# Four of eight channel tiles of a depthwise convolution: taps from VectorE to GpSimd

## The chip, the cores and the metric

One core of a Trainium2 chip runs the whole kernel. The metric is the device time of one execution in microseconds; lower is better. The engines are TensorE (PE in the profile; its weight loads are PEld), VectorE (DVE), ScalarE (ACT), GpSimd (POOL) and SyncE (SP). Each works through its own queue of instructions in order; semaphores order them against each other.

## The reference

One encoder layer on 512 tokens of width 1024, in float32:

```python
h = rms_norm(x, norm_mix_pre)
za, zb, q, k, v, su, sv, gl = split(h @ w_in)
a = za * sigmoid(zb)                          # the gated input of the convolution
a = depthwise_conv(a, conv_w, conv_b)         # 31 taps along the tokens, one filter a channel
y_a = silu(layer_norm(a, conv_ln_g, conv_ln_b)) @ w_proj_conv
y_b = rms_norm(diff_attention(q, k, v)) @ w_proj_attn        # 8 heads, two softmaxes each
y_c = (gelu(su) * spatial(layer_norm(gelu(sv)))) @ w_proj_sgu
g_a, g_b, g_c = split(sigmoid(gl + b_gate))
x = x + rms_norm((g_a*y_a + g_b*y_b + g_c*y_c) @ w_out)
x = x + rms_norm(relu(rms_norm(x) @ w_ffn_up)**2 @ w_ffn_down)
```

## The kernel before

All matrices are multiplied in three products of split operands: each float32 operand is a rounded part (`_hi`, written by ScalarE, L150) and the rest (`_lo`, subtracted by VectorE, L151), and hi x hi, hi x lo and lo x hi are summed. A *unit* is one 128 x 512 result over 1024 inputs: 24 products. Weights come by SyncE's queue, are split two units ahead of their use (`take`, `load_to`) and are kept in three buffers.

The order of TensorE is the order of the program (`keep_in_program_order`). The other engines' queues are ordered when the kernel is built, by a planner that follows dependences and a priority, which is the place in the program unless it is changed.

The stages that matter here, in TensorE's order:

1. The rows of x are normalized and turned; the first gated tiles (`glu`, 0 and 1) are made.
2. Attention, eight heads. A head makes scores for four groups of 128 tokens, and for each VectorE writes the combined probabilities `at` (L515); TensorE turns them, and ScalarE and VectorE split them into `ath` and `atl` (L72), which the product with the values reads. Between these steps run the next head's queries and keys (`kk`, L465) and the other six gated tiles (2 to 7).
3. The normalized and gelu'd half of the spatial gating unit (`sv_half`, `gv_norm`), with its two rows `sg_g` and `sg_b` and its weights `wraw` loaded through GpSimd's queue; the projection of attention; the spatial gating unit, which writes `sh` and `sl`; its projection, which reads them.
4. The convolution's norm (`conv_norm`: TensorE turns `apad`, ScalarE writes the normalized rows `y`), its silu, its projection, which writes `mh` and `ml`; then the output product and the feed-forward half.

The convolution has the channels on partitions, in eight tiles of 128 channels: `apad` holds a tile's 512 tokens with 15 zeros on either side. VectorE writes a gated tile into it (`glu_out`, L396). A tile's convolution is 31 instructions on VectorE, one after the other on one accumulator: the last tap with the bias (L367), then 30 fused multiply-and-add instructions (L372), the last of which writes over the start of the tile's own row. They are one generator over all tiles, `taps`; `conv(n, behind)` issues the next n of them after a given instruction, with a priority lowered by 3000. `glu_out` asks for 11 taps (`CONVG`), later hooks for 5, 14, 3 and 9 at a time.

Buffers named by the same tag in the same pool share a place. `sh` and `mh` are both `bh` in the pool `brp`; `y` has four buffers of its own in `p3`.

Of the kernel before, what the change touches and what calls it, by code (L numbers as in the profile page):

```python
# [8 lines left out]
F32 = mybir.dt.float32  # L9
F32R = mybir.dt.float32r  # L10
AF = mybir.ActivationFunctionType
ALU = mybir.AluOpType
# [4 lines left out]
P = 128  # L17
S = 512
D = 1024
KT = D // P  # L20
TT = S // P
# [3 lines left out]
CK = 31  # L25
PAD = 15
# [12 lines left out]
CONVG = 11  # L39
# [9 lines left out]
def encoder_layer(ctx: ExitStack, tc: tile.TileContext, a: dict, out: bass.AP):  # L49
    nc = tc.nc  # L50
    vec, act, pool = nc.vector, nc.scalar, nc.gpsimd
# [12 lines left out]
    def mk(name, bufs=1, **kw):  # L64
        return tc.tile_pool(name=name, bufs=bufs, reuse_waits="tile", **kw)
# [104 lines left out]
    def bank(tag):  # L170
        return ps["pool"].tile([P, 512], F32, tag=tag, bufs=ps[tag], name=f"ps_{tag}")
# [97 lines left out]
    with mk("p0") as p0:  # L269
# [76 lines left out]
        convw = cq.tile([P, KT, 32], F32, tag="convw", name="convw")  # L346
        vec.tensor_copy(convw, b[:, P:P + KT * 32].rearrange("p (k j) -> p k j", j=32))

        def pc(n, i=0):
            return pcol[:, col[n] + i:col[n] + i + 1]  # L350
# [6 lines left out]
    cvp = big.enter_context(mk("cvp"))  # L357
    apad = cvp.tile([P, KT, S + 2 * PAD], F32, tag="apad", name="apad")
# [2 lines left out]
    pad(big, "pad3", 64)  # L361
    mixp = big.enter_context(mk("mixp"))

    def conv_taps():
        for c in range(KT):
            acc = cvp.tile([P, S], F32, tag="acc", name="acc")
            vec.tensor_scalar(acc, apad[:, c, CK - 1:CK - 1 + S], convw[:, c, CK - 1:CK], pc("conv_b", c),  # L367
                              op0=ALU.mult, op1=ALU.add)
            yield
            for j in range(CK - 2, -1, -1):  # L370
                o = acc if j else apad[:, c, 0:S]
                vec.scalar_tensor_tensor(o, apad[:, c, j:j + S], convw[:, c, j:j + 1], acc,  # L372
                                         op0=ALU.mult, op1=ALU.add)
                yield

    taps = conv_taps()

    def conv(n, behind):

        with tc.issue_after(behind.ins):  # L380
            keep = tc.cur_priority
            tc.cur_priority = keep + LOWP
            for _ in range(n):
                next(taps, None)
            tc.cur_priority = keep + (tc.cur_priority - keep - LOWP)
# [7 lines left out]
        return sg  # L393

    def glu_out(c, ba, sg):
        conv(CONVG, vec.tensor_tensor(apad[:, c, PAD:PAD + S], ba, sg, op=ALU.mult))  # L396

    def glu(c, p):
        wb, wa = take(2)
        bb = bank("a")  # L400
        yield from unit_gen(bb, wb, hT)
        sg = glu_gate(bb, p)
        ba = bank("a")
        yield from unit_gen(ba, wa, hT)
        glu_out(c, ba, sg)

    glu_out(0, fb[1], glu_gate(fb[0], ap_))
    sg1 = glu_gate(fb[2], ap_)
    (w,) = take(1)
    b = bank("a")  # L410
    unit(b, w, hT)
    glu_out(1, b, sg1)
    for c in range(2, KT - GLU_LATE):
        run(glu(c, ap_))
# [3 lines left out]
    for i in (1, 2):  # L418
        lq = bcast(ap_, f"lq{i}", a[f"lam_q{i}"], 64)
        lk = bcast(ap_, f"lk{i}", a[f"lam_k{i}"], 64)  # L420
        pr = ap_.tile([P, 64], F32, tag="lpr", name="lpr")
# [164 lines left out]
    brp = big.enter_context(mk("brp"))  # L586
# [28 lines left out]
    bh = brp.tile([P, KT, S], F32R, tag="bh", name="bh")  # L615
# [17 lines left out]
    def ln_stats(p, parts):  # L633
        st = p.tile([P, 2, 6], F32, tag="st", bufs=4, name="st")
        for i, s in enumerate(parts):
            vec.bn_stats(st[:, i], s)
        mv = p.tile([P, 2], F32, tag="mv", bufs=4, name="mv")
        vec.bn_aggr(mv, st)
        r = rstd_of(p, mv[:, 1:2], 1.0)
        nb = p.tile([P, 1], F32, tag="nb", bufs=4, name="nb")  # L640
        vec.scalar_tensor_tensor(nb, mv[:, 0:1], -1.0, r, op0=ALU.mult, op1=ALU.mult)
        return mv, r, nb
# [96 lines left out]
    p3 = c3.enter_context(mk("p3"))  # L739
    ch = p3.tile([P, KT, S], F32R, tag="ch", name="ch")  # L740
    cl = p3.tile([P, KT, S], F32R, tag="cl", name="cl")
    ys = []

    def conv_norm(t):
        bs = [bank("b") for _ in range(2)]
        for c in range(KT):
            pe.transpose(bs[c // 4][:, (c % 4) * P:(c % 4 + 1) * P], apad[:, c, t * P:(t + 1) * P], ident)
        mv, r, nb = ln_stats(p3, bs)
        y = p3.tile([P, D], F32, tag="y", bufs=4, name="y")
        for i in range(2):  # L750
            act.activation(y[:, i * 512:(i + 1) * 512], bs[i], AF.Identity, bias=nb, scale=r)  # L751
        ys.append(y)

    def conv_silu(c):
        b = bank("b")
# [9 lines left out]
    for n in range(EARLY):  # L765
        (wg,) = take(1)
        ga.append(gate(p3, wg, 0, n, "ga", EARLY))
        if NORM <= n < NORM + 2:
            conv_norm(2 * (n - NORM))
            conv_norm(2 * (n - NORM) + 1)  # L770
        elif NORM + 2 <= n < NORM + 4:
            for c in range(4 * (n - NORM) - 8, 4 * (n - NORM) - 4):
                conv_silu(c)
# [377 lines left out]
    for q in range(1, FT // 4):  # L1151
# [15 lines left out]
        ba = bank("a")  # L1167
# [48 lines left out]
    ba = [bank("a") for _ in range(2)]  # L1216
# [45 lines left out]
    for n, step in enumerate(seq[:-TAIL]):  # L1262
# [4 lines left out]
        p_, i = step  # L1267
# [48 lines left out]
def build(arrays):  # L1316
    import concourse.bacc as _bacc

    nc = _bacc.Bacc("TRN2", target_bir_lowering=False, num_devices=1)
    args = {}  # L1320
    for n in _INS:
        a = arrays[f"in_{n}_dram"]
        args[n] = nc.dram_tensor(f"in_{n}_dram", a.shape, mybir.dt.from_np(a.dtype), kind="ExternalInput").ap()
    out = nc.dram_tensor("out_0_dram", (S, D), F32, kind="ExternalOutput").ap()
    with tile.TileContext(nc) as tc:
        encoder_layer(tc, args, out)
    return nc
# [10 lines left out]
```

## Time and profile before

| | us |
|---|---|
| Median of 3 runs | 1060.08 (1059.95 to 1060.1) |
| The profiled execution | 1059.99 |
| Its span, first to last instruction | 1058.2 |
| Busy: PE / DVE / ACT / POOL | 1042.6 / 827.0 / 580.5 / 24.3 |
| All taps of L372 that write the accumulator, 232 | 173.5 |
| First and last gated tile written (L396) | 38.7 and 307.8 |
| First transpose of `apad` | 597.8 |

In the profile's rows a time is followed by the engine, the line of the kernel, the operation and `out<-in` by the program's names, with the shapes; in brackets stands how long the engine had been idle and what it waited for. A row by stretch gives the stretch, its length, and busy time with the number of instructions of PE, PEld, DVE, ACT and POOL, then the granted clock, the share of the DMA engines and their GB/s; where it was asked for one line of the kernel it has that engine's time alone. A row of a line's instructions gives the shortest, median and longest duration in ns and the first and last start.

### The profile page before, as it was taken

How to read it: one execution, taken by the hardware profiler on the slowest of the kernel's cores; microseconds unless marked ns; L12 is line 12 of the kernel's file. 1: busy time of each engine (PE TensorE's matmuls, PEld its weight loads, DVE VectorE, ACT ScalarE, POOL GpSimd, SP SyncE). 2: the span in 40 equal slices, each digit the busy share in tenths (PEclk: the TensorE clock that was granted, in tenths of full speed). 3: DMA queues.
4: the chain of work that ended last, by engine and by line, in shares of the span. 5: the costliest groups of instructions: out<-in, count | busy, mean ns of one | idle time of the engine just before them, and what ended most of it. 6: DMA issues, size and time to landing. Idle time of an engine off the chain costs nothing.

```text
span 1058.2 us, 14724 instructions
## 1 busy us (share of the span) xinstructions
PE 1042.6 (99%) x5688; PEld 900.0 (85%) x5688; DVE 827.0 (78%) x1296; ACT 580.5 (55%) x902; POOL 24.3 (2%) x41
## 2 busy tenths in 40 slices
PE   8999999999999999999999999999999999999997
PEld 7989898888878888888888888888999999888885
DVE  6696887968997697999899546457988889867746
ACT  5456677766673752344322493344677787555531
POOL 3000000000000000000000000000000001100000
PEclk9999999999999999999999999999999999999999
DMA  7342323223232333322333214463343319724532
GB/s 227 84 139 61 100 81 100 80 81 87 73 120 87 92 112 90 99 81 80 100 100 99 80 45 135 132 226 138 112 150 101 122 43 265 150 80 139 178 121 80
DMA packets 138391, 118.15 MB, mean 112 GB/s; under 512 B 4166, under 2 KB 116850, under 8 KB 138321
## 3 DMA queue, kind: packets, MB, share of 16 engines
q1 hardware_dynamic: 133120, 103.82, 32.1%
q0 software_dynamic: 4480, 11.82, 4.8%
q10 hardware_dynamic: 720, 1.57, 0.4%
q8 instruction: 44, 0.72, 0.3%
q14 instruction: 27, 0.21, 0.1%
HBM read 108.81 MB, written 4.19 MB: 107 GB/s over the span
## 4 chain that ended last, share of the span: by engine, by line
PE 91%; DVE 5%; ACT 2%; issue 1%; DMA 1%; DVEq 0%; ACTq 0%
PE ps_a L58 69%; PE ps_b L58 19%; PE ps_b L62 3%; DVE w_lo L951 1%; DMA xx<-in_x_dram 1%; DVE us L1257 0%; DVE w_lo L151 0%; ACT y L751 0%; DVE hs L303 0%; DVE jk L827 0%; PE ps_a L62 0%; DVE hl L224 0%; ACT jk L825 0%; DVE jk L1247 0%; DVE rs_s L206 0%
## 5 line engine op out<-in xcount | busy, mean ns | idle before, releaser
L150 ACT ACTIVATE w_hi<-w_raw 128x1024 fp32r<-128x1024 f32 x116 | 122.9, 1059 | 214.0 <-PE ps_a L58 177.4
L58 PE MATMUL ps_a<-hh,w_hi 128*128 128x512 f32 (+1 forms) x536 | 205.4, 385 | 0.0
L58 PE MATMUL ps_a<-hh,w_lo 128*128 128x512 f32 (+1 forms) x536 | 202.9, 381 | 0.0
L58 PE MATMUL ps_a<-hl,w_hi 128*128 128x512 f32 (+1 forms) x536 | 202.5, 380 | 0.0
L372 DVE SCALAR_TENSOR_TENSOR acc<-apad,convw,acc 128x512 f32<-128x512 f32 x232 | 173.5, 748 | 5.0
L151 DVE TENSOR_TENSOR w_lo<-w_raw,w_hi 128x1024 fp32r<-128x1024 f32 x116 | 141.5, 1220 | 41.5 <-ACT w_hi L150 41.2
L58 PEld LDWEIGHTS ps_a<-hh,w_lo 128*128 128x128 f32 x536 | 100.3, 188 | 19.6
L58 PEld LDWEIGHTS ps_a<-hl,w_hi 128*128 128x128 f32 x536 | 100.4, 188 | 18.3
L58 PEld LDWEIGHTS ps_a<-hh,w_hi 128*128 128x128 f32 x536 | 100.4, 188 | 18.2
L58 PE MATMUL ps_a<-ring,w_hi 128*128 128x256 f32 x336 | 57.9, 276 | 0.0
L58 PEld LDWEIGHTS ps_a<-ring,w_hi 128*128 128x128 f32 x336 | 50.6, 188 | 0.0
L58 PE MATMUL ps_a<-h2h,w_lo 128*128 128x256 f32 x176 | 48.8, 277 | 1.4 <-DVE w_lo L951 1.4
L58 PE MATMUL ps_a<-w_hi,hh 128*128 128x256 f32 (+1 forms) x160 | 49.7, 311 | 0.0
L58 PE MATMUL ps_a<-h2h,w_hi 128*128 128x256 f32 x176 | 49.0, 278 | 0.0
L58 PE MATMUL ps_a<-h2l,w_hi 128*128 128x256 f32 x176 | 48.8, 277 | 0.0
L58 PE MATMUL ps_a<-w_hi,hl 128*128 128x256 f32 (+1 forms) x160 | 48.7, 304 | 0.0
L58 PE MATMUL ps_a<-w_lo,hh 128*128 128x256 f32 (+1 forms) x160 | 48.6, 304 | 0.0
L507 ACT ACTIVATE e<-ps_b,m 128x512 f32<-128x512 f32 x64 | 43.4, 681 | 7.3 <-DVE m L503 7.0
L58 PE MATMUL ps_a<-ring,w_lo 128*128 128x256 f32 x168 | 46.5, 277 | 0.2 <-DVE w_lo L951 0.2
L58 PE MATMUL ps_a<-w_hi,ring 128*128 128x512 f32 x144 | 45.5, 389 | 0.0
L503 DVE CUSTOM_DVE_ANT_0 ps_b<-ps_b,al 128x512 f32<-128x512 f32 x64 | 43.5, 698 | 0.5 <-PE ps_b L58 0.2
L951 DVE TENSOR_TENSOR w_lo<-w_raw,w_hi 128x1024 fp32r<-128x1024 f32 x28 | 33.7, 1220 | 8.3 <-ACT w_hi L947 8.3
(304 smaller groups left out, 2431.6 us busy)
## 6 DMA issues: line engine op xcount, KB each, us to landing
w_raw<-in_w_in_dram SPq DMA_DIRECT2D x80, 512.0 KB, 3.7
w_raw<-in_w_ffn_up_dram SPq DMA_DIRECT2D x32, 512.0 KB, 4.6
w_raw<-in_w_ffn_down_dram SPq DMA_DIRECT2D x28, 512.0 KB, 4.1
w_raw<-in_w_proj_attn_dram SPq DMA_DIRECT2D x8, 512.0 KB, 4.0
w_raw<-in_w_proj_sgu_dram SPq DMA_DIRECT2D x8, 512.0 KB, 4.1
w_raw<-in_w_proj_conv_dram SPq DMA_DIRECT2D x8, 512.0 KB, 4.1
w_raw<-in_w_out_dram SPq DMA_DIRECT2D x8, 512.0 KB, 3.6
t<-in_w_ffn_down_dram SPq DMA_DIRECT2D x8, 512.0 KB, 5.7
```

The costliest lines, as they stand in the source:

```text
L58: return tc.keep_in_program_order(nc.tensor.matmul(*args, **kw))
L62: return tc.keep_in_program_order(nc.tensor.transpose(*args, **kw))
L150: act.activation(hi, raw, AF.Copy)
L151: vec.tensor_tensor(lo, raw, f32(hi[:, :]), op=ALU.subtract)
L372: vec.scalar_tensor_tensor(o, apad[:, c, j:j + S], convw[:, c, j:j + 1], acc, op0=ALU.mult, op1=ALU.add)
L503: vec.tensor_tensor_reduce(b, b, nal[:, 384 - q * P:896 - q * P], 1.0, 3.0e38, ALU.add, ALU.min, m)
L507: act.activation(e, b, AF.Exp, bias=m, scale=-1.0, accum_out=l)
L951: order(vec.tensor_tensor(lo, raw, f32(hi[:, :]), op=ALU.subtract))
```

## The change

The taps of tiles 1, 3, 5 and 7 are issued to GpSimd instead of VectorE, all 31 as soon as the gated tile is written, at the priority of their place in the program. GpSimd has a product with a scalar per partition and, as another instruction, a sum: 31 products (the first with the bias) and 30 sums a tile, with an accumulator and one buffer for the product in the convolution's pool. The generator keeps the other four tiles, and `conv` still asks for as many taps at each place. The normalized rows `y` of the convolution's norm are no longer four buffers in `p3` but one tile in the place of `sh`, tag `bh`.

```diff
+    POOLED = (1, 3, 5, 7)
+
+    def tile_taps(c):
+        acc = cvp.tile([P, S], F32, tag="acc", name="acc")
+        vec.tensor_scalar(acc, apad[:, c, CK - 1:CK - 1 + S], convw[:, c, CK - 1:CK], pc("conv_b", c),
+                          op0=ALU.mult, op1=ALU.add)
+        yield
+        for j in range(CK - 2, -1, -1):
+            o = acc if j else apad[:, c, 0:S]
+            vec.scalar_tensor_tensor(o, apad[:, c, j:j + S], convw[:, c, j:j + 1], acc,
+                                     op0=ALU.mult, op1=ALU.add)
+            yield
+
+    def pool_taps(c):
+
+        acc = cvp.tile([P, S], F32, tag="pacc", name="acc")
+        pool.tensor_scalar(acc, apad[:, c, CK - 1:CK - 1 + S], convw[:, c, CK - 1:CK], pc("conv_b", c),
+                           op0=ALU.mult, op1=ALU.add)
+        for j in range(CK - 2, -1, -1):
+            pr = cvp.tile([P, S], F32, tag="ppr", name="pr")
+            pool.tensor_scalar(pr, apad[:, c, j:j + S], convw[:, c, j:j + 1], None, op0=ALU.mult)
+            pool.tensor_tensor(acc if j else apad[:, c, 0:S], acc, pr, op=ALU.add)
+
     def conv_taps():
         for c in range(KT):
-            ...
+            if c not in POOLED:
+                yield from tile_taps(c)
...
     def glu_out(c, ba, sg):
-        conv(CONVG, vec.tensor_tensor(apad[:, c, PAD:PAD + S], ba, sg, op=ALU.mult))
+        i = vec.tensor_tensor(apad[:, c, PAD:PAD + S], ba, sg, op=ALU.mult)
+        if c in POOLED:
+            pool_taps(c)
+        conv(CONVG, i)
...
         mv, r, nb = ln_stats(p3, bs)
-        y = p3.tile([P, D], F32, tag="y", bufs=4, name="y")
+        if not ys:
+            yt = brp.tile([P, TT, D], F32, tag="bh", name="y")
+            ys.extend(yt[:, t_] for t_ in range(TT))
+        y = ys[t]
         for i in range(2):
             act.activation(y[:, i * 512:(i + 1) * 512], bs[i], AF.Identity, bias=nb, scale=r)
-        ys.append(y)
```

More of the change, by code (lines that the diff above doesn't have):

```diff
@@ L362, in encoder_layer @@
     mixp = big.enter_context(mk("mixp"))
+    POOLED = (1, 3, 5, 7)
[17 more added lines that the diff above has]
+            pool.tensor_tensor(acc if j else apad[:, c, 0:S], acc, pr, op=ALU.add)
     def conv_taps():
         for c in range(KT):
[L366 to L374, printed above, removed]
+            if c not in POOLED:
+                yield from tile_taps(c)
     taps = conv_taps()
```

## The prediction

> **What bounds the kernel now.** I read the page's busy times first, then TensorE's busy time by stage, then TensorE's own waits up to the end of the convolution, then the timelines of VectorE around the taps.
>
> ```profile
> span 1058.2 us, 14724 instructions
> ...
> PE 1042.6 (99%) x5688; PEld 900.0 (85%) x5688; DVE 827.0 (78%) x1296; ACT 580.5 (55%) x902; POOL 24.3 (2%) x41
> L372 DVE SCALAR_TENSOR_TENSOR acc<-apad,convw,acc 128x512 f32<-128x512 f32 x232 | 173.5, 748 | 5.0
> 0.00:38.00 38.00, 33.23 (x223) 29.75 (x224) 20.66 (x42) 18.62 (x29) 9.01 (x24) 1.00 0.64 186
> 38.00:390.00 352.00, 350.86 (x1820) 298.40 (x1819) 294.64 (x606) 230.84 (x433) 2.00 (x3) 1.00 0.32 92
> 390.00:620.00 230.00, 229.71 (x1058) 190.62 (x1057) 190.88 (x271) 83.70 (x106) 0.00 (x0) 1.00 0.31 90
> PE ps_b L62 <- ACT oT L535: 0.7, 1, 0.7
> PE ps_b L58 <- DVE kk L465: 0.4, 1, 0.4
> PE ps_b L62 <- ACT y L751: 0.3, 1, 0.3
> ```
>
> The busy share of VectorE (78%) invites one to relieve it; the stage rows say what that is worth. In them the third number is TensorE's busy time. From 38 to 620 us, the whole stretch in which taps or their readers run, TensorE stands still for 1.14 + 0.29 = 1.43 us, at a granted clock of 1.00. Its three waits there come to the same 1.4 us, and none names a tap. The other 14 us of idle time lie ahead of 38 us and behind 620 us, where there are no taps. So TensorE is the bound, and what the change can gain in this stretch ends at 1.43 us.
>
> **The change, part by part.** Four tiles of 31 taps leave VectorE: by the row of L372, about 4 x 31 x 0.748 = 93 us of its time. Where do they leave it?
>
> ```profile
> 40.00:66.00 26.00, 15.70 (x21) 1.00 0.37 108
> 450.00:590.00 140.00, 77.87 (x104) 1.00 0.31 91
> 450.00:590.00 140.00, 125.92 (x163) 1.00 0.31 91
> 42.25 0.69 DVE L396 TENSOR_TENSOR apad<-ps_a,sg 128x512 f32<-128x512 f32 x1 [0.37 <-PE ps_a L58]
> 185.16 0.69 DVE L396 TENSOR_TENSOR apad<-ps_a,sg 128x512 f32<-128x512 f32 x1 [0.76 <-PE ps_a L58]
> 277.23 0.69 DVE L396 TENSOR_TENSOR apad<-ps_a,sg 128x512 f32<-128x512 f32 x1 [0.76 <-PE ps_a L58]
> 307.75 0.69 DVE L396 TENSOR_TENSOR apad<-ps_a,sg 128x512 f32<-128x512 f32 x1
> ```
>
> The first two rows are the taps of L372 alone, the third is all of VectorE. The code still hands out 11 taps behind each of the eight gated tiles, so up to 310 us VectorE runs the 88 steps it runs now, only of other tiles. What is left, 36 steps, is used up soon after; the relief falls on the stretch from 450 us, where 104 taps vanish from 126 us of work while TensorE has no idle time to give back. Gain there: 0, with an end at -1.4 us (all three waits gone).
>
> What is added lies on GpSimd: 31 products and 30 sums of 128x512 for each of four tiles, starting when L396 has written tile 1, 3, 5 and 7 (the four rows above: 42.9, 185.9, 277.9, 308.4 us). No such instruction is in the trace; the nearest rows are these:
>
> ```profile
> 0.95 0.20 POOL L331 MEMSET prow<- 128x128 f32 x1
> 4.76 0.97 POOL L338 MEMSET cw<- 32x1024 f32 x1
> 1.19 0.29 POOL masks.py:199 TENSOR_SCALAR_AFFINE_SELECT ident<-ident 128x128 f32<-128x128 f32 x1
> L62 PE MATMUL ps_b<-ident,apad x32: 270/272/273, 597.8 to 606.6; 128*128 128x128 f32 x32
> ```
>
> Writing grows by (0.97 - 0.20)/896 = 0.86 ns an element, so 512 are written in 0.20 + 384 x 0.86 ns = 0.53 us: the lower end for either instruction. Reading 128 elements adds 0.09 us, so 512 add 0.36: a product comes to 0.89, a sum with two inputs to 1.25 us. The upper end is the 0.29 us in proportion, 1.16 for a product and, read twice, 2.32 for a sum. A tile: 31 x 0.89 + 30 x 1.25 = 65 us (32 to 106). I take 65, since those rates separate start from stream. Then tile 1 runs from 43 to 108 us, tile 3 from 186 to 251, tiles 5 and 7 one behind the other from 278 to 408 (at the upper end to 490). The first reader of all tiles, the transposes of the convolution's norm, stands at 597.8 us: at least 108 us of cover, and the cost of the taps' own length is 0. It would cost one for one from (597.8 - 277.9)/122 = 2.6 us an instruction on.
>
> The unknown is what GpSimd's reads do to VectorE beside them. A tap there reads two SBUF tensors, as do w_lo (L151) and at (L515). Lower end: nothing. Upper end: each such VectorE instruction waits for a whole GpSimd instruction, 65/61 = 1.07 us. No row has a GpSimd instruction that reads a tensor beside a busy VectorE (its memsets read none), so none is near either end; I take the middle, 0.53 us for each, and look for the places where TensorE has less cover than that adds up to.
>
> ```profile
> 62.93 0.73 DVE L372 SCALAR_TENSOR_TENSOR acc<-apad,convw,acc 128x512 f32<-128x512 f32 x1
> 64.42 0.75 DVE L372 SCALAR_TENSOR_TENSOR acc<-apad,convw,acc 128x512 f32<-128x512 f32 x1
> 65.51 1.22 DVE L151 TENSOR_TENSOR w_lo<-w_raw,w_hi 128x1024 fp32r<-128x1024 f32 x1 [0.34 <-ACT w_hi L150]
> 122.19 0.69 DVE L72 TENSOR_TENSOR atl<-ps_b,ath 128x512 fp32r<-128x512 f32 x1 [0.45 <-ACT ath L71]
> 124.34 0.39 PE L58 MATMUL ps_b<-atl,vh 128*128 128x512 f32 x1
> 300.00:310.00 10.00, 10.00 (x49) 8.27 (x48) 10.00 (x15) 6.76 (x9) 0.00 (x0) 1.00 0.33 106
> 298.85 0.74 DVE L515 SCALAR_TENSOR_TENSOR at<-e,c,at 128x512 f32<-128x512 f32 x1
> 301.02 0.75 DVE L515 SCALAR_TENSOR_TENSOR at<-e,c,at 128x512 f32<-128x512 f32 x1
> 301.69 2.35 DVE L151 TENSOR_TENSOR w_lo<-w_raw,w_hi 128x1024 fp32r<-128x1024 f32 x2
> 306.43 0.68 DVE L72 TENSOR_TENSOR atl<-ps_b,ath 128x512 fp32r<-128x512 f32 x1
> 307.79 0.39 PE L58 MATMUL ps_b<-atl,vh 128*128 128x512 f32 x1
> ```
>
> Place one, the first keys (kk, L465): TensorE already waits 0.4 us for them, so there is no cover. Ahead of kk in VectorE's queue stand three two-input instructions: 3 x 0.53 - 0.34 of idle time = 1.25 us (0 to 3 x 1.07 = 3.2). Place two, the last turned quarter of a usual head: atl ends at 122.88, its reader starts at 124.34, a cover of 1.46 us, and VectorE even idles ahead of it; 0. Place three, the last head, while tile 5 is on GpSimd: atl ends at 307.11, its reader starts at 307.79, a cover of 0.68, and VectorE has no idle time at all (10.00 of 10 us). At, at and two w_lo are in front: 4 x 0.53 - 0.68 = 1.45 us; the taps in between have the lowest priority and can be put behind. Lower end 0; if the six or so taps are not put behind, 10 x 1.07 - 0.68 = 10 us. Elsewhere each weight is split two units ahead of its use, which hides a microsecond.
>
> By the Trainium skill (SBUF — State Buffer, Who interferes with whom), VectorE with two SBUF inputs and a GpSimd instruction that reads SBUF exclude each other for the whole instruction. By that rule the wait is what is left of a running GpSimd instruction, about half of one, and the sum is the same 2.7 us; if the two engines did not meet at all it would be 0. No run here shows it yet. The skill (GPSIMD Engine Reference, Performance versus the Vector engine) gives 4497 ns for a sum of 2048 elements; a quarter of that, 1.1 us, is an estimate that speaks for my 1.25.
>
> GpSimd's queue also issues DMAs, and the taps join them. The lambda rows and the iota are ready before tile 1 is. The sgu norm's two rows and the sgu weights (wraw) come due while tiles 5 and 7 run:
>
> ```profile
> 310.74 0.55 POOL L187 DMA_DIRECT2D sg_g<-in_sgu_ln_g_dram x1 [283.85 <-PE ps_b L58]
> 370.46 0.92 POOL L696 DMA_DIRECT2D wraw<-in_sgu_w_dram x1 [58.56 <-DVE gvl L650]
> DMA to landing us min/median/max: 4.5/4.5/4.5
> L62 PE MATMUL ps_b<-ident,wraw x8: 270/272/273, 435.2 to 436.0; 128*128 128x128 f32 x8
> 317.90 0.18 DVE L209 TENSOR_TENSOR rs_s<-rs_s,rs_r 128x32 f32<-128x32 f32 x1
> 318.02 0.75 DVE L372 SCALAR_TENSOR_TENSOR acc<-apad,convw,acc 128x512 f32<-128x512 f32 x1
> 318.69 0.17 DVE L210 TENSOR_SCALAR rs_s<-rs_s 128x32 f32<-128x32 f32 x1
> ```
>
> The last three rows show how the planner treats a chain whose links depend on each other: a tap of lower priority gets in between two links. So I expect a DMA that is ready to get in between two taps of GpSimd's chain, and not behind the chain. If it does stand behind both chains, wraw is issued at 277.9 + 122 x 1.07 = 408 us; it has to be by 435.2 - 4.5 - 0.9 = 429.8. Covered, at a cost of 0; behind the wait of the sgu DMAs only taps queue, and those have 190 us.
>
> The normalized rows (y) move into the place of sh. That adds one wait, of y's first write for the last product that reads sh:
>
> ```profile
> L58 PE MATMUL ps_a<-sh,w_lo x64: 389/389/389, 505.7 to 586.7; 128*128 128x512 f32 x64
> L751 ACT ACTIVATE y<-ps_b,nb,rs_r x8: 770/779/786, 603.3 to 612.8; 128x512 f32<-128x512 f32 x8
> ```
>
> sh is read out 16 us before y is written, and mh, next in that place, is written only after TensorE has turned y, as its program order has it. Cost 0; without that cover, ScalarE would hold up the norm by what is missing.
>
> **Sum.** 0 (relief) + 0 (length) + 1.25 (first keys) + 1.45 (last head) + 0 (DMAs) + 0 (y) = +2.7 us. The profiled execution took 1059.99 us, 1.8 more than its span, and stands 0.1 under the median of 1060.08. From the median: 1062.8 us. About 0.2%, 2.1 us, is what a measurement here can tell from no change, so this is barely slower.
>
> **The rivals.** *No change, 1060.1 us (1058.7 to 1062.1).* The engines' reads do not hold each other up, or the planner shifts the taps so that both tight places keep their cover. For it: 99% TensorE, and only two places of such thin cover in 580 us. Against it: keys that TensorE waits for already. It decides where the delay per instruction stays under 0.4 us: 3 x 0.4 - 0.34 + 4 x 0.4 - 0.68 = 1.8.
>
> *GpSimd too slow for its queue, 1085 us.* The order of the queue is fixed beforehand. If 87 tap instructions stand ahead of wraw, as 1.07 us each would give ((370.5 - 277.9)/1.07), it is late from (429.8 - 277.9)/87 = 1.75 us an instruction on; at 2.0 us it is issued at 452, and the eight transposes wait 22 us with all of TensorE behind them. For it: every tap may also wait for VectorE, which was busy up to 10 of 10 us. Against: 59 us between need and issue.
>
> *Faster, 1057.5 us.* The relieved VectorE takes more than the 1.43 us out of TensorE's idle time, by weights and gates coming earlier than the waits show. Against: there is no more idle time at those lines, and the relief lies where TensorE is full.
>
> **How the numbers follow.** Forecast 0.43 (own range 1062.2 to 1071.4, the last with place three's 10 us), no change 0.40, late queue 0.10, faster 0.07. Slower by over 0.2% is the first and the third, 0.53; within 0.2% 0.40; faster 0.07. The range leaves out most of the late queue and most of faster: 1058.9 to 1072.
>
> **What would show it.** TensorE's waits between 60 and 70 us and between 295 and 312 us: if kk and atl (or at) stand there with a microsecond or more, the sum's two terms are right; if they are as before, the rival of no change is. VectorE's w_lo and taps: longer than 1.22 and 0.75 us, or with gaps ahead of them, inside the four GpSimd stretches and not outside, would show that the reads exclude each other. GpSimd's length per tile (65 us) and the issue of wraw (before 430 us) test the cover. VectorE's busy time from 450 to 590 us should fall by some 78 us with TensorE's the same. The prediction is wrong in sign if TensorE's idle time from 38 to 620 us falls, and wrong in size if a new wait there exceeds 5 us, or if the y rows or the transposes of the norm wait.

## The result, and the profile after

The changed kernel takes 1166.21 us (median; 1163.77 to 1167.2) where the kernel before takes 1060.01 on the same chip: a ratio of 1.0985, with a 95% interval of 1.0963 to 1.1008. It is 106 us slower; the forecast was 2.7 us slower (1062.8), and the upper end of the range 1072. Executions of one kernel fall on two levels some 4 us apart (1060.2 and 1064.3 us for the kernel before), and a rare one that is far slower stays out of the ratios.

The page of the changed kernel (the last four lines are its groups of instructions: busy time and mean ns of one, then the idle time ahead of them):

```profile
span 1165.4 us, 14849 instructions
...
PE 1065.0 (91%) x5688; PEld 909.6 (78%) x5688; DVE 827.7 (71%) x1172; ACT 581.2 (50%) x902; POOL 442.4 (38%) x285
...
L384 POOL TENSOR_SCALAR pr<-apad,convw 128x512 f32<-128x512 f32 x120 | 241.4, 2012 | 11.4
L385 POOL TENSOR_TENSOR acc<-acc,pr 128x512 f32<-128x512 f32 x116 | 166.5, 1435 | 9.6
L151 DVE TENSOR_TENSOR w_lo<-w_raw,w_hi 128x1024 fp32r<-128x1024 f32 x116 | 157.5, 1358 | 97.8 <-ACT w_hi L150 97.5
L373 DVE SCALAR_TENSOR_TENSOR acc<-apad,convw,acc 128x512 f32<-128x512 f32 x116 | 128.2, 1105 | 2.0
```

VectorE lost half of its taps and is as busy as before, 827.7 us against 827.0. A tap takes 1105 ns (748 before) and a split of a weight 1358. TensorE's idle time grew from 1058.2 - 1042.6 = 15.6 us to 1165.4 - 1065.0 = 100.4, by 85; its busy time, for the same 5688 matmuls, grew by another 22. Together that is the whole 107 us of the span. By stage (PE, PEld, DVE, ACT, POOL busy, then the granted clock) and by wait (us in total, how often, the longest):

```profile
38.00:390.00 352.00, 322.91 (x1629) 268.43 (x1628) 320.91 (x542) 200.61 (x397) 280.18 (x166) 0.97 0.27 77
390.00:620.00 230.00, 173.22 (x755) 141.17 (x754) 125.78 (x142) 74.58 (x91) 139.89 (x82) 0.87 0.24 71
```

```profile
PE ps_a L58 <- DVE w_lo L151: 36.5, 5, 27.9
PE ps_b L62 <- DMA wraw<-in_sgu_w_dram: 21.2, 1, 21.2
PE ps_b L58 <- DVE w_lo L151: 5.7, 2, 5.3
PE ps_b L58 <- DVE kk L484: 4.8, 1, 4.8
PE ps_b L58 <- DVE atl L72: 4.8, 4, 2.7
```

TensorE stood still for 1.4 us from 38 to 620 us before; now for 29 up to 390 us, mostly in attention, and 57 behind that. Two waits of 28 and 21 us stand out, and a crowd of waits of 1 to 5 us for VectorE.

**The two long waits** are read in the timeline, engine by engine (start, duration, instruction, and the idle time with its cause):

```profile
427.07 1.26 POOL L385 TENSOR_TENSOR acc<-acc,pr 128x512 f32<-128x512 f32 x1
428.43 1.56 POOL L384 TENSOR_SCALAR pr<-apad,convw 128x512 f32<-128x512 f32 x1
429.94 0.59 POOL L187 DMA_DIRECT2D sg_g<-in_sgu_ln_g_dram  x1
...
434.06 2.31 DVE L666 TENSOR_TENSOR gv<-gv,sg_g 128x1024 f32<-128x1024 f32 x1 [28.71 <-DMA sg_g<-in_sgu_ln_g_dram]
...
440.29 0.80 PE L58 MATMUL ps_a<-hh,w_lo 128*128 128x512 f32 x1 [27.93 <-DVE w_lo L151]
...
535.80 0.99 POOL L715 DMA_DIRECT2D wraw<-in_sgu_w_dram  x1
...
540.24 1.97 PE L62 MATMUL ps_b<-ident,wraw 128*128 128x128 f32 x8 [21.15 <-DMA wraw<-in_sgu_w_dram]
```

The load of sg_g, issued at 310.7 before, is issued at 429.9. It stands behind tiles 1, 3, 5 and the first eight instructions of tile 7. VectorE reaches its reader, stops there for 28.7 us, and behind that reader in its queue is the split of a weight that TensorE needs: the wait is put down to w_lo, but a DMA is its cause. wraw stands behind the last tap of the last tile and comes at 535.8. In 427 to 430 us VectorE is standing still, so these two rows are GpSimd's own durations: 1.56 us for a product, 1.26 for a sum.

**The short waits.** VectorE ahead of the first keys in the kernel before (rows of 62 to 66 us stand in the prediction):

```profile
52.55 2.31 DVE L372 SCALAR_TENSOR_TENSOR acc<-apad,convw,acc 128x512 f32<-128x512 f32 x3
...
57.38 3.89 DVE L372 SCALAR_TENSOR_TENSOR acc<-apad,convw,acc 128x512 f32<-128x512 f32 x5
...
66.77 0.68 DVE L465 TENSOR_TENSOR kk<-ps_a,kk 64x512 fp32r<-64x512 f32 x1
```

The same in the changed kernel, with TensorE behind it:

```profile
57.27 3.52 DVE L373 SCALAR_TENSOR_TENSOR acc<-apad,convw,acc 128x512 f32<-128x512 f32 x3
...
64.08 5.54 DVE L373 SCALAR_TENSOR_TENSOR acc<-apad,convw,acc 128x512 f32<-128x512 f32 x5
69.54 2.32 DVE L151 TENSOR_TENSOR w_lo<-w_raw,w_hi 128x1024 fp32r<-128x1024 f32 x1
...
76.35 0.69 DVE L484 TENSOR_TENSOR kk<-ps_a,kk 64x512 fp32r<-64x512 f32 x1
...
77.09 0.80 PE L58 MATMUL ps_b<-kk,qh 128*128 128x512 f32 x1 [4.83 <-DVE kk L484]
```

Eight taps take 9.1 us where they took 6.2, a split 2.3 instead of 1.2, and VectorE has no idle time to make it up. The keys come at 76.4 instead of 66.8 us. They themselves read one tensor from PSUM and take 0.69 us as before. In the last head TensorE waits for `atl` twice, 1.3 and 2.7 us:

```profile
339.67 0.80 PE L58 MATMUL ps_b<-atl,vh 128*128 128x512 f32 x1 [2.68 <-DVE atl L72]
```

The 5.3 us wait has another kind of instruction ahead of it. First the row of before, then those of after:

```profile
326.12 4.59 DVE L623 TENSOR_SCALAR ob<-ob,rs_r 128x128 f32<-128x128 f32 x23
```

```profile
367.69 10.88 DVE L642 TENSOR_SCALAR ob<-ob,rs_r 128x128 f32<-128x128 f32 x23
378.48 1.21 DVE L151 TENSOR_TENSOR w_lo<-w_raw,w_hi 128x1024 fp32r<-128x1024 f32 x1
...
379.75 0.79 PE L58 MATMUL ps_b<-w_lo,hh 128*128 128x512 f32 x1 [5.28 <-DVE w_lo L151]
```

Twenty-three scalings of the attention rows, 0.20 us each before, take 0.47 us each. They have one tensor as input, so two tensor inputs are not needed for being held up. Whether their length alone makes the wait is taken up with the experiments.

**The busier TensorE** shows in the granted clock behind a wait, here behind that for the keys:

```profile
74.00:78.00 4.00, 0.91 (x2) 0.50 (x2) 3.31 (x4) 1.34 (x3) 3.82 (x3) 0.85 0.73 204
78.00:80.00 2.00, 1.87 (x5) 1.28 (x5) 1.44 (x4) 0.78 (x2) 1.90 (x2) 0.50 0.72 213
...
82.00:84.00 2.00, 2.00 (x7) 1.59 (x6) 1.27 (x2) 0.89 (x1) 1.82 (x3) 0.58 0.00 0
84.00:86.00 2.00, 2.00 (x10) 1.62 (x9) 1.87 (x3) 1.43 (x4) 1.90 (x2) 1.00 0.11 26
```

After a wait of 4.8 us the clock is at one half for about 6 us. The same matmul takes 0.63 us there and 0.39 from 84 us on. So a wait of five microseconds costs some three more. TensorE's busy time multiplied by the missing part of the clock, summed over stretches of 1 us up to 620 us, comes to 16 of the 22 us by which its busy time grew; the other 6 were not followed.

### The profile page after: what moved, and what is told of

It is laid out like the page before. It is cut to its first block, busy times and chain, and to the rows that moved or that the text cites. A ratio compares the mean times of both kernels' runs of the same rounds, so it can differ in the third digit from the quotient of the medians.

```text
span 1165.4 us, 14849 instructions
## 1 busy us (share of the span) xinstructions
PE 1065.0 (91%) x5688; PEld 909.6 (78%) x5688; DVE 827.7 (71%) x1172; ACT 581.2 (50%) x902; POOL 442.4 (38%) x285
## 4 chain that ended last, share of the span: by engine, by line
PE 48%; DVE 4%; ACT 2%; issue 1%; DMA 0%; DVEq 0%; ACTq 0%
PE ps_a L58 36%; PE ps_b L58 11%; PE ps_b L62 1%; DVE w_lo L972 1%; DVE us L1278 0%; DMA wraw<-in_sgu_w_dram 0%; ACT y L773 0%; DVE jk L848 0%; ACT jk L846 0%; DVE jk L1268 0%; DVE wk L843 0%; DVE w_sum L960 0%; ACT rs_s L201 0%; DVE st L655 0%; DVE rs_s L206 0%
## 5 line engine op out<-in xcount | busy, mean ns | idle before, releaser
L384 POOL TENSOR_SCALAR pr<-apad,convw 128x512 f32<-128x512 f32 x120 | 241.4, 2012 | 11.4
L58 PE MATMUL ps_a<-hh,w_lo 128*128 128x512 f32 (+1 forms) x536 | 207.3, 389 | 36.5 <-DVE w_lo L151 36.5
L151 DVE TENSOR_TENSOR w_lo<-w_raw,w_hi 128x1024 fp32r<-128x1024 f32 x116 | 157.5, 1358 | 97.8 <-ACT w_hi L150 97.5
L58 PE MATMUL ps_a<-hh,w_hi 128*128 128x512 f32 (+1 forms) x536 | 209.4, 393 | 1.2 <-ACT w_hi L150 1.2
L58 PE MATMUL ps_a<-hl,w_hi 128*128 128x512 f32 (+1 forms) x536 | 206.3, 387 | 0.0
L385 POOL TENSOR_TENSOR acc<-acc,pr 128x512 f32<-128x512 f32 x116 | 166.5, 1435 | 9.6
L58 PEld LDWEIGHTS ps_a<-hh,w_lo 128*128 128x128 f32 x536 | 102.8, 193 | 59.2 <-DVE w_lo L151 38.7
L373 DVE SCALAR_TENSOR_TENSOR acc<-apad,convw,acc 128x512 f32<-128x512 f32 x116 | 128.2, 1105 | 2.0
L58 PEld LDWEIGHTS ps_a<-hh,w_hi 128*128 128x128 f32 x536 | 102.8, 193 | 20.6 <-ACT w_hi L150 1.6
L1057 POOL DMA_DIRECT2D t<-in_w_ffn_down_dram x8 | 9.6, 1197 | 174.3 <-DVE w_lo L1104 153.8
```

What stands on the lines that cost most here:

```text
L58: return tc.keep_in_program_order(nc.tensor.matmul(*args, **kw))
L151: vec.tensor_tensor(lo, raw, f32(hi[:, :]), op=ALU.subtract)
L384: pool.tensor_scalar(pr, apad[:, c, j:j + S], convw[:, c, j:j + 1], None, op0=ALU.mult)
L385: pool.tensor_tensor(acc if j else apad[:, c, 0:S], acc, pr, op=ALU.add)
L1057: pool.dma_start(sum_at(n, i).rearrange("p (k c) -> p k c", c=512), rows("w_ffn_down", 2 * i, 512), accum_op=ALU.add)
```

## The experiments

My theory after the result had two parts: the three loads in GpSimd's queue come late (Q1), and GpSimd's reads lengthen VectorE's instructions (Q2). The rivals were that the place of y or the mere load on GpSimd does it, and later, within Q2, whether the held-up instructions or those queued behind them are what costs. Times are to be held against 1060.2 to 1060.6 us for the kernel before on the same chips.

**The loads alone, moved to SyncE's queue.**

```diff
-        pool.dma_start(t, src.partition_broadcast(P))          # sg_g, sg_b
+        nc.sync.dma_start(t, src.partition_broadcast(P))
-            pool.dma_start(wraw...)
+            nc.sync.dma_start(wraw...)
```

> The changed kernel with the three DMAs of the spatial gating unit (its two norm rows and its weights) issued by SyncE's queue instead of GpSimd's; the taps stay on GpSimd. Theory A (two causes: the DMAs queue behind taps that run longer than the planner took them for, and GpSimd's and VectorE's reads exclude each other): the waits of 27.9 and 21.2 us go, and most of the lower clock with them; the waits of the attention stay, so 1085 to 1105 us. Rival B (the exclusion does nearly all of it, VectorE simply runs out of time): the waits reappear on w_lo, above 1140 us. Rival C (only the queue): 1060 to 1066 us.

Measured: 1119.61 us, a ratio of 1.0542 (1.0503 to 1.0581). Both long waits are gone. The short ones are as they were, but for one of 5.1 us for a split, at 442.8 us, where the long waits stood:

```profile
PE ps_a L58 <- DVE w_lo L151: 13.6, 5, 5.1
PE ps_b L58 <- DVE w_lo L151: 5.9, 2, 5.3
...
PE ps_b L58 <- DVE kk L484: 4.8, 1, 4.8
```

So the queue cost 46.6 us, about what the two waits show (27.9 and 21.2). The 59 us that stay are more than I had expected.

**The place of y alone** (`POOLED = ()`: all taps on VectorE, y in the place of sh).

> The changed kernel with no tile on GpSimd: all taps on VectorE as before, only the normalized rows in the place of sh (and the two small buffers' room). Theory A: 1060 us, within 2 us. Rival D (the moved rows or the shifted buffers cost something by themselves): over 1063 us, with a wait before y's first write or at mh.

Measured: 1062.33 us, ratio 1.0007 (0.9989 to 1.0024). The ratio counts here, not the median; and TensorE is busy for 350.86 and 229.70 us in the two stretches, as before the change. The move of y costs nothing.

**GpSimd's load beside VectorE's full taps, reading and not reading.** All 248 taps stay on VectorE, whose results the output uses; GpSimd works on scratch rows, and the loads are on SyncE's queue.

```diff
 # reading: same number of products and sums a tile
-            pool.tensor_scalar(pr, apad[:, c, j:j + S], convw[:, c, j:j + 1], None, op0=ALU.mult)
-            pool.tensor_tensor(acc if j else apad[:, c, 0:S], acc, pr, op=ALU.add)
+            pool.tensor_scalar(pr, acc, convw[:, c, j:j + 1], None, op0=ALU.mult)
+            pool.tensor_tensor(acc, acc, pr, op=ALU.add)
 # not reading
+        for _ in range(90):
+            pool.memset(scr, 0.0)          # 128 x 1024
```

> All taps on VectorE, the three DMAs on SyncE's queue, and GpSimd runs the same 61 products and sums a tile beside them on a scratch accumulator that nobody reads: GpSimd's reads alone, VectorE's work unchanged. Theory A: VectorE's two-input instructions grow as in the changed kernel (w_lo from 1.22 to 1.5 us, taps from 0.75 to 1.1 us in those stretches) and TensorE waits; with no relief of VectorE, 1090 to 1130 us. Rival C (only the queue costs): 1060 to 1066 us.

> As the run with reads beside, but GpSimd writes zeros to a scratch tile instead, 90 memsets of 128x1024 a tile (90 x 0.97 = 87 us): GpSimd as busy, at the same places, but reading nothing. Theory A: VectorE's durations stay 1.22 and 0.75 us and the time is that of before, 1058 to 1063 us. Rival E (a busy GpSimd as such holds VectorE up, by its writes or its queue): near the run with reads beside.

Measured, one run each: 1138.71 us with reads, above the range expected, and 1060.85 with memsets. The groups of the first and of the second:

```profile
L373 DVE SCALAR_TENSOR_TENSOR acc<-apad,convw,acc 128x512 f32<-128x512 f32 x232 | 229.9, 991 | 5.0
L151 DVE TENSOR_TENSOR w_lo<-w_raw,w_hi 128x1024 fp32r<-128x1024 f32 x116 | 158.9, 1370 | 36.7 <-ACT w_hi L150 36.5
```

```profile
L382 POOL MEMSET scr<- 128x1024 f32 x360 | 344.8, 958 | 20.7
L373 DVE SCALAR_TENSOR_TENSOR acc<-apad,convw,acc 128x512 f32<-128x512 f32 x232 | 173.5, 748 | 5.0
L151 DVE TENSOR_TENSOR w_lo<-w_raw,w_hi 128x1024 fp32r<-128x1024 f32 x116 | 141.4, 1219 | 36.1 <-ACT w_hi L150 35.9
```

345 us of memsets leave VectorE's taps and splits, which have two tensors as input, at their durations of before; reads lengthen them. For these Q2 holds: it is what GpSimd reads, not that it is busy. The Trainium skill (SBUF — State Buffer, Who interferes with whom) says just that: VectorE with two SBUF inputs contends with a GpSimd instruction that reads, not with one that only writes.

The scalings, with one tensor as input, are another case: the memsets hold them up too. All 32 of them (busy time, then mean ns), before the change and beside memsets:

```profile
L623 DVE TENSOR_SCALAR ob<-ob,rs_r 128x128 f32<-128x128 f32 x32 | 6.5, 278 | 0.0
L638 DVE TENSOR_SCALAR ob<-ob,rs_r 128x128 f32<-128x128 f32 x32 | 16.7, 923 | 0.0
```

In the changed kernel their mean is 583 ns. So for them it is not GpSimd's reads alone. Beside the memsets the 23 scalings ran from 328.0 to 340.2 us, and TensorE waited 0.3 us for the split behind them: their length alone does not make the wait of 5.3 us.

**A shorter product.** A product with a second operation (+ 0.0) runs in a faster form.

```diff
-            pool.tensor_scalar(pr, ..., None, op0=ALU.mult)
+            pool.tensor_scalar(pr, ..., 0.0, op0=ALU.mult, op1=ALU.add)
```

> The changed kernel with each product written as a product and a sum with 0.0 in the one instruction, as the first tap is (0.76 us there undisturbed, against 1.56 us of the plain product); the same values, DMAs still in GpSimd's queue. Theory F (the plain product alone has a slow form): a product takes 0.75 us undisturbed, a tile 31 x 0.8 + 30 x 1.36 = 65 us undisturbed and some 80 us beside VectorE, the two norm rows come some 40 us earlier, and the time falls to 1095 to 1125 us. Rival G (the second 0.8 us is a wait for the sum before, which read the same product buffer): the product stays at 1.56 us and the time at 1166 us.

Measured: 1133.16 us, ratio 1.0681 (1.0645 to 1.0716). The product's mean fell from 2012 to 1166 ns; sg_g is issued at 401.8 and wraw at 490.7, and neither holds TensorE up any more. The step is as expected, the time above it.

**The shorter product and the moved loads together.**

> The products of the run before and the three DMAs on SyncE's queue. Theory A and F (what is left is the exclusion of reads, in proportion to GpSimd's reading time): the 59 us over before of the run with moved DMAs shrink with GpSimd's busy time, to 25 to 45 us: 1085 to 1105 us. Rival (the exclusion counts instructions, not time): near 1120 us.

Measured: 1135.08 us, ratio 1.0699 (1.066 to 1.0738): no better than the shorter product alone, and worse than the moved loads alone (1119.6). This expectation missed. GpSimd was busy for 94 us less (352.5 us), yet a tap of VectorE took 1089 ns and a split 1363, about as with the moved loads alone (1105 and 1384).

**Half the count, the same elements.** As the reading run above, with 15 products and 15 sums of 128x1024 a tile.

> As the run in which GpSimd works on scratch rows beside VectorE's full 248 taps (1138.7 us), but 15 products and 15 sums of 128x1024 a tile in place of 30 and 30 of 128x512: half as many GpSimd instructions, as many elements. If the price goes by the number of instructions (each hands VectorE's next instruction one wait): the 78 us halve, 1095 to 1110 us. If it goes by the time in which GpSimd reads: 1128 to 1145 us, as before. If single waits of 2 to 3 us are worse than many short ones: above 1145 us.

Measured: 1137.63 us, ratio 1.0717 (1.0674 to 1.0761), against 1138.7. So the price does not go by the number of GpSimd's instructions, nor by its busy time, which fell from 447.0 to 350.2 us. The elements read were the same, and in the run before this one, too; that they set the price is not shown, since the run before this one cost 15 us more than the moved loads alone at the same elements.

**One tile only** (`POOLED = (7,)`, loads moved).

> The DMAs on SyncE's queue, the plain product, and only tile 7 on GpSimd, from 308 to some 415 us, behind the attention. Theory A (a delay costs only where TensorE has little cover, above all in the attention and where weights are split just in time): 1062 to 1075 us, with w_lo waits of some us between 360 and 400. Rival (cost in proportion to tiles): a quarter of 59 us, 1075 us or above.

Measured: 1085.09 us, ratio 1.0228 (1.0189 to 1.0266). This is above my range, and a quarter of the GpSimd work costs more than a quarter of the 59 us: 25. Its longest wait, 5.3 us, is the one behind the 23 scalings. They took 10.9 us, less than beside the memsets, but began at 335.6 instead of 328.0 us: what stood ahead of them in VectorE's queue had come late, and that had used up the cover. Whether the taps of another tile would be cheaper, no run shows.

**Later, where VectorE looked relieved.** Tiles 5 and 7 only, started when the projection of attention has written its fourth block (a copy of one element of it comes first); shorter product, loads moved.

```diff
-    POOLED = (1, 3, 5, 7)
+    POOLED = (5, 7)
...
+        if n == TT:                        # in the hook beside the projection
+            for c in POOLED:
+                pool_taps(c)
```

> The DMAs on SyncE's queue, products of two operations, and tiles 5 and 7 alone on GpSimd, started only when the projection of attention has written its fourth block (some 405 us): past the attention and the spatial gating unit's norm, two tiles one behind the other, done by about 560 us, ahead of the norm at 597. Theory A: VectorE's instructions still grow beside them, but TensorE has cover there: 1060 to 1067 us, no better than before since TensorE was full. Rival B (VectorE short of time wherever GpSimd reads): over 1075 us, with w_lo waits there.

Measured: 1111.6 us, ratio 1.0478 (1.0455 to 1.0501). My theory here, that this stage has cover, fell: TensorE waited 23.3 us for the mix (six times) and 16.5 for w_lo. VectorE's own taps are there too, at 974 ns each.

That pointed at what the runs so far had in common: VectorE's low-priority taps in the same stretch. Three runs ask for them; all have the loads on SyncE's queue.

**Without VectorE's taps.** The four tiles of VectorE are left out of the computation; GpSimd's four stay.

```diff
-                yield from tile_taps(c)
+                yield from ()
```

> The changed kernel with the three DMAs on SyncE's queue (that alone: 1119.6 us) and without VectorE's own four tiles of taps, which are left out of the computation; GpSimd's four tiles stay. Theory Q (VectorE's order was laid out with taps of 0.75 us; each takes 1.1 us beside GpSimd's reads, and the split of a weight or the keys that stand behind such taps in the same queue come late by the sum): without the taps most of the 59 us go: 1062 to 1078 us, and the waits of TensorE for w_lo come to less than 5 us in all. Theory D (the splits, keys and probabilities are held up by GpSimd's reads directly, taps or not): 1095 to 1115 us, with w_lo still at some 1.4 us and its waits above 12 us.

Measured: 1072.34 us, ratio 1.0105 (1.0073 to 1.0137). GpSimd's reads go on, a split still takes 1347 ns, but the waits for it come to 4.6 us:

```profile
PE ps_a L58 <- DVE w_lo L151: 2.4, 1, 2.4
PE ps_b L58 <- DVE w_lo L151: 2.2, 1, 2.2
```

So 47 of the 59 us need VectorE's taps beside GpSimd's reads; all 248 taps without GpSimd's reads cost nothing (the runs with y alone and with memsets), and GpSimd's reads without the taps cost the other 12. The run takes away the taps' place in the queue together with all their work, so it does not tell the two apart. That the place counts is argued from the rows: with the loads moved, VectorE was busy for 320.7 of the 352 us from 38 to 390 us, so it was not out of time on the whole.

**VectorE's taps later** (`CONVG = 0`: none behind the gated tiles, all by the later hooks; nothing left out).

> The changed kernel with the three DMAs on SyncE's queue and no VectorE taps handed out behind the gated tiles (11 each before): VectorE's four tiles are computed in full from the projection of attention on, by the later hooks. Theory Q: during attention as without VectorE's taps, so 1062 to 1085 us; what is left lies behind 390 us, where the taps now meet GpSimd's tiles 5 and 7. Theory D: 1095 to 1120 us.

Measured: 1103.46 us, ratio 1.0398 (1.0374 to 1.0422). That lies in the rival's range, not in mine. By stage:

```profile
38.00:390.00 352.00, 344.87 (x1785) 291.78 (x1784) 265.52 (x504) 223.79 (x426) 286.99 (x181) 1.00 0.31 89
390.00:620.00 230.00, 206.59 (x884) 167.93 (x883) 195.35 (x204) 65.50 (x80) 116.89 (x63) 0.94 0.28 80
```

In attention, where no tap of VectorE runs now, TensorE works 345 of 352 us (323 in the changed kernel). So the rival's cause, reads that need no taps, accounts for 7 us of standing still there; the other 23 came behind 390 us, where the taps went while GpSimd still worked. The timeline there has the pattern in two rows:

```profile
436.55 7.16 DVE L373 SCALAR_TENSOR_TENSOR acc<-apad,convw,acc 128x512 f32<-128x512 f32 x6
443.64 1.21 DVE L151 TENSOR_TENSOR w_lo<-w_raw,w_hi 128x1024 fp32r<-128x1024 f32 x1
```

Six taps of 1.2 us stand in the queue ahead of a split; six of 0.75 would have let it start 2.7 us earlier.

**Kept apart in time.** Shorter product; VectorE's taps handed out from the spatial gating unit on (3 behind each of its eight tiles, 18 behind each unit of its projection).

> The whole computation with the two engines' taps kept apart in time: the three DMAs on SyncE's queue, GpSimd's product written with a second operation (+ 0.0; with both of these and VectorE's taps where they were: 1135.1 us), and VectorE's four tiles handed out only from the spatial gating unit on (3 behind each of its eight tiles, 18 behind each unit of its projection), when GpSimd should be through. Theory Q: without VectorE's taps beside GpSimd the time was 1072.3; with shorter products and the taps in a stretch without GpSimd's reads, where one takes 0.75 us and VectorE has room (126 of 140 us were busy there with 104 taps before the change), 1060 to 1072 us. Rival (GpSimd's reads hold up splits, keys and probabilities by themselves, and shorter products make VectorE alternate with GpSimd as often as before): 1075 to 1090 us. In neither can it come out more than 1.4 us under the kernel before, since TensorE has no more idle time there.

Measured: 1102.88 us, ratio 1.0401 (1.0378 to 1.0423). Above both expectations. Its waits, and its counterpart to the 23 scalings with GpSimd beside them:

```profile
PE ps_b L62 <- DVE apad L373: 17.8, 1, 17.8
PE ps_b L58 <- DVE w_lo L151: 8.2, 1, 8.2
```

```profile
333.76 13.32 DVE L642 TENSOR_SCALAR ob<-ob,rs_r 128x128 f32<-128x128 f32 x23
...
335.92 0.74 POOL L384 TENSOR_SCALAR pr<-apad,convw 128x512 f32<-128x512 f32 x1
336.75 1.33 POOL L385 TENSOR_TENSOR acc<-acc,pr 128x512 f32<-128x512 f32 x1
```

17.8 us are a mistake of this experiment: away from GpSimd a tap takes 750 ns again, but pushed this far back the last one ends at 638 us, when the norm already waits for it. The rest, some 25 us, I put down to GpSimd's reads by themselves, by subtraction alone; it is more than the 12 us with the longer product and no taps (8.2 us of waiting behind the scalings, 2.2 there). The rows suggest why: product and sum follow each other every 2.2 us instead of every 3.1, and the 23 scalings take 13.3 us instead of 10.9. A pair of product and sum held VectorE up by (10.88 - 4.59)/3.5 = 1.8 us with the long product and by (13.32 - 4.59)/5.9 = 1.5 with the short one. The shorter instruction comes more often and saves VectorE little, which fits that the shorter product brought nothing once the loads were moved.

No version with taps on GpSimd that computes the whole layer came near the kernel before: the nearest, with tile 7 alone, is 25 us slower. The most that any could gain in this stretch was the 1.43 us that TensorE stood still.

## Why the prediction was wrong

**Right.** TensorE is the bound and relief of VectorE is worth 0. The length of GpSimd's chain costs nothing by itself: the last tile ended at 535.8 us, and no run with GpSimd's taps showed a wait of the norm for them. The move of y costs 0. The sum's mechanism, two-input instructions of VectorE held up by GpSimd's reads, is there, at both places named: the keys and the last head's atl.

**The step on the DMAs failed, at 0 for 46.6 us.** "I expect a DMA that is ready to get in between two taps of GpSimd's chain": it does get in between two taps, but at a place in the queue that was fixed when the kernel was built. sg_g stands behind 69 tap instructions that follow the writing of tile 5 at 277.9; to be due at 310.7 as before, each may have been counted at no more than 32.8/69 = 0.48 us. That is inferred from the order; no run shows the planner's prices. On the chip one takes 107/61 = 1.75 (tile 5, from 311.8 to 418.7 us). Even the fallback, behind all chains, was costed with 1.07 us an instruction and for wraw alone. "Behind the wait of the sgu DMAs only taps queue" was wrong as well: a split of a weight queued there, and that was the longest wait of all. The rival of the late queue had the mechanism and was given 0.10. That its 22 us for wraw's wait meets the 21.2 measured is luck: it put the issue at 452 us for a need at 430, while the load was issued at 535.8, behind all the chains, for a need that had itself come late, at 519.

**The durations on GpSimd.** The sum was right (1.25; 1.26 measured), the product wrong (0.89; 1.56 undisturbed, 2.01 on the mean). It had been put together from the growth of memsets and the reading of 128 elements by another instruction. A tile took 107 us (tile 5), not 65, just past the upper end of 106. That made the loads later: with the shorter product they hold nothing up. For the other term the shorter product brought nothing.

**The terms of the held-up instructions: 2.7 us for 59.** At the two places counted, the keys cost a wait of 4.8 us (0.4 before) where 1.25 were forecast, and the last head's atl 4.0 where 1.45 were. Yet the delay of one instruction was not too small on the mean: 0.53 us assumed; a tap gained 0.36, a split 0.14 (the one ahead of the keys 1.1). What failed was the count of places and of what stands ahead at each. "Elsewhere each weight is split two units ahead of its use, which hides a microsecond": TensorE waited seven times for a split, once of these for the late load. The delays do not stand singly but add up in an in-order queue, with three to six taps ahead of a split in the rows above, and "the taps in between have the lowest priority and can be put behind" holds only while the queue is planned; on the chip a tap of the lowest priority delays whatever stands behind it. The run without VectorE's taps puts 47 us on taps beside GpSimd's reads; that it is by their place in the queue is read from the rows, as said above. The prediction took that microsecond for granted everywhere but at its two places and did not look at what the planner had queued ahead of the other splits.

**Too few instructions were counted.** Only two tensor inputs were taken to meet GpSimd's reads. The scalings, with one, went from 0.20 to 0.47 us. The section of the Trainium skill that the prediction cites has the sentence for it (SBUF — State Buffer, Who interferes with whom): a tensor_scalar can run in a mode that uses both ports and then contends with GpSimd. The traces agree in that these are held up, beside memsets too (923 ns for 278); that the mode is the reason, no run here shows. The prediction had used the other sentence alone.

**The clock was not in the sum.** By the sum above, 16 of the 107 us are matmuls at a lower granted clock behind waits.

## What to carry to other kernels

Before moving work to an idle engine, look at what its queue already issues: a load placed behind slow instructions waits for all of them, and the wait may show up under another engine's name. On an engine whose queue is filled with low-priority work, a longer instruction is not paid once but by everything queued behind it; so take the cover from the queue (what stands ahead of the next instruction that TensorE needs), not from the busy share. And where TensorE has no idle time, relief of another engine has nothing to win.

## What the runs showed of the hardware

- GpSimd's product of 128x512 with a scalar per partition takes 1.56 us with one operation and 0.74 to 0.76 with a second one (+ 0.0, or the bias), with VectorE out of the way or not hindering it.
- Its memsets (958 ns for 128x1024) left VectorE's taps and splits, with two tensors as input, as they were (748 and 1219 ns) and held up two kinds with one: 278 became 923 ns for a scaling of 128x128, and 542 became 692 ns, on the mean of eight, for the tap with the bias.
- Its reads lengthened the taps and splits (991 and 1370 ns) and the scalings (583). Half as many instructions of twice the length cost as much (1137.6 and 1138.7 us). That the two shorter-product runs end above the moved loads alone (1135 and 1133 against 1119.6) is explained above only for one place; where the rest of those 15 us arises was not followed.
- A wait of TensorE of 4.8 us was followed by a granted clock of 0.50 for about 6 us, the same matmul taking 0.63 instead of 0.39 us. The Trainium skill (TensorE: Matmul & The Clock Gate, What's actually happening) gives half the clock after an idle window of about 3.4 us. The trace agrees for that wait, but shorter ones go both ways: 2.14 us (59.8 to 62.0) were followed by 0.50 from some 63.3 to 66.4 us, and 1.67 us (146.1 to 147.8) left the clock at 1.00. No run here tells the window's length.
